# A two-layer streaming-encoder trunk: the norm's g applied with tokens on partitions, and latents normalised token tile by token tile

## The chip, the cores and the metric

The kernel runs on one core of a Trainium2 chip. The metric is the device time of one execution in microseconds (us); before the change its median over three runs is 704.25 us (703.63 to 704.76). The engines have their own instruction queues and meet through semaphores: TensorE (PE; its weight loads are listed as PEld), VectorE (DVE), ScalarE (ACT), GpSimd (POOL) and SyncE (SP), which here issues the DMAs.

## The reference

The input x is 512 tokens of 1024 numbers, float32. Each of two layers computes

```
h = rmsnorm(x) * norm_g[l]                       # over the 1024 features
p = split(h @ w_in[l])                           # 4040 columns
o_a = latent attention(p.a_cq, p.a_ckv, p.a_krope)
o_b = differential attention;  o_c = attention on the top 128 keys of an indexer;  o_d = short gated convolution
x = x + concat(o_a*silu(gate_a), o_b*..., o_c*..., o_d*...) @ w_out[l]
```

and at the end x is normalised once more, with final_g. In the latent attention the 256 columns a_cq and the 128 columns a_ckv of each token are normalised by their own root mean square, multiplied by their own g, and then by the small matrices w_uq (256 x 384) and w_ukv (128 x 512) to give queries, keys and values. The indexer needs 40 further columns of the same projection (one key of 32 and eight weights), and a_krope has 32.

## The kernel before

Products keep nearly full precision by splitting each operand into a high part (rounded by ACT's copy to the matmul's type) and a low part (the difference, by DVE or POOL), and adding three matmuls: high by high, high by low, low by high (`mm3`, L122). A helper on the way out of PSUM, `split_ps` (L112), does such a split with one ACT and one DVE instruction; `split_w` (L103) does it for a weight in SBUF with one ACT cast and subtractions of 256 columns on POOL.

Norm. `Norm` (L250) holds one tile of 128 tokens, tokens on partitions. `part` sums squares on ACT, `finish` makes the reciprocal root (ACT Sqrt, then a few DVE steps on 128x1) and multiplies the two halves of 512 columns, one on DVE (L287) and one on ACT (L288). In the layers g is not applied there: `Hidden.fill` (L296) transposes the tile to features on partitions, 128 by 128, eight times, two to a PSUM bank, and each 128-column split multiplies by g, which then is one number per partition (`gcol`, got by transposing norm_g once, L991 to L993). Only the final norm has g on tokens: POOL multiplies x by it early (L274).

First stage. Each layer begins with the 456 columns that the latents and the indexer need: for token tile t and weight quarter q, `first_part(q, t)` adds six matmuls into the tile's PSUM bank (tiles 0 and 1 in banks named proj, of which there are three, tiles 2 and 3 in banks named s). The order of norms (n), fills (e), weight splits (c) and parts is written out in `FIRST`. After quarter 3 ACT copies the bank to SBUF (L517, tile t1s).

Latents. `latent` (L583) then copies the indexer's columns out, sums the squares of all four tiles' latents (L599, L600), takes one reciprocal root over 128x8 numbers by integer steps on DVE (`rsqrt`, L136), multiplies (L608), transposes the latents (L616), splits them with their g per partition, builds the rotary key, loads and splits w_ukv (L647 to L655), multiplies by it (L656 on), then loads and splits w_uq and multiplies by that (L670 on). These matmuls are listed under L127 (`mm3`). `latent` runs merged with the first projections of the indexer and gates (`merge`, L229): the generators yield estimated costs, and the stream that is least far goes next, which fixes the program order.

Order and buffers. SP's order in the first stage of layer 0 is the written one. Elsewhere and on all other engines a planner orders instructions by readiness in its own cost model, earlier program order first, and hands out buffers from pools: 20 buffers of 512 KB named big, four raw weight buffers (`raw_tile`), four for split weights, seven named prob.

At the end of layer 0, `out_last` adds the last products to x, and `after` runs the next layer's norm and fills on each token tile beside it.

Of the kernel before, what the change touches and what calls it, by code (L numbers as in the profile page):

```python
# [19 lines left out]
P = 128  # L20
S = 512
D = 1024
# [43 lines left out]
def hybrid_trunk(ctx, tc, x_in, norm_g, w_in, qa_g, w_uq, kva_g, w_ukv, dlam, subg,  # L66
# [91 lines left out]
    grow = const.tile([DEPTH * KT, P], FT, name="grow")  # L158
    gcol = const.tile([P, DEPTH * KT], FT, name="gcol")
# [85 lines left out]
    def load_g(src):  # L245
        g = flat(big(FT))
        nc.sync.dma_start(g, src[None, :].to_broadcast([P, D]))
        return g

    class Norm:  # L250


        def __init__(self, x, g=None):
            self.x, self.g = x, g
            self.xn = flat(big(FT))
            self.ss = sm.tile([P, 4], FT, name="ss")
            self.n = 0

        def part(self, c):
# [11 lines left out]
            if self.g is not None:  # L271
# [4 lines left out]
        def finish(self):  # L276
# [9 lines left out]
            src = self.x if self.g is None else xn  # L286
            nc.vector.tensor_scalar(out=xn[:, :512], in0=src[:, :512], scalar1=r, scalar2=None, op0=OP.mult)  # L287
            nc.scalar.activation(xn[:, 512:], src[:, 512:], AF.Copy, scale=r)  # L288

    class Hidden:  # L290
        def __init__(self, l):
            self.l0 = l * KT
# [3 lines left out]
        def fill(self, t, xn):  # L296
            for g in range(4):
                b = bank("pt")
                for j in range(2):
                    k = 2 * g + j  # L300
                    nc.tensor.transpose(b[:, j * P:(j + 1) * P], xn[:, k * P:(k + 1) * P], ident)
                    split_ps(self.h[g][:, j, t * P:(t + 1) * P], self.l[g][:, j, t * P:(t + 1) * P],
                             b[:, j * P:(j + 1) * P], gcol[:, self.l0 + k:self.l0 + k + 1])
# [6 lines left out]
    def layer(l, hT, enter, after):  # L310
# [182 lines left out]
        t1s = [big(FT), big(FT)]  # L493
        t1 = lambda t, c0, c1: t1s[t // 2][:, t % 2, c0:c1]
# [14 lines left out]
        def first_part(q, t):  # L509
# [6 lines left out]
            if q == 3:  # L516
                nc.scalar.copy(t1(t, 0, 456), acc[t][:, :456])  # L517
# [64 lines left out]

        def latent():  # L583
            rep = prob()
            repv = rep.rearrange("p (t r c) -> p t r c", t=NT, r=4)
            for i in range(2):
                nc.vector.tensor_copy(repv[:, 2 * i:2 * i + 2],
                                      t1s[i][:, :, None, 416:448].to_broadcast([P, 2, 4, 32]))
            widx = A["widx"] = sm.tile([P, NT, 8], FT, name="widx", bufs=2)
            for i in range(2):  # L590
                nc.vector.tensor_copy(widx[:, 2 * i:2 * i + 2], t1s[i][:, :, 448:456])
# [4 lines left out]
            ss = sm.tile([P, NT, 2], FT, name="ssa")  # L596
            for t in range(NT):
                jk = prob()
                nc.scalar.activation(jk[:, :256], t1(t, 0, 256), AF.Square, accum_out=ss[:, t, 0:1])  # L599
                nc.scalar.activation(jk[:, 256:384], t1(t, 256, 384), AF.Square, accum_out=ss[:, t, 1:2])  # L600
# [485 lines left out]
```

## Time and profile before

| | before |
|---|---|
| median of three runs | 704.25 us |
| the profiled execution's own time | 706.75 us |
| its span, first to last instruction | 705.0 us |
| mean granted TensorE clock | 0.969 |
| PE / PEld busy | 637.8 / 538.9 us |
| DVE / ACT / POOL busy | 490.3 / 382.3 / 275.7 us |

The rest of this document reads one profiled execution. "Busy" is time in which an engine executes; register, branch and semaphore instructions don't count. Matmul ends are modelled, so a busy PE is not necessarily PE at its peak. The granted clock is the share of full speed that PE was given. A wait is put down to the semaphore that came last.

### The profile page before, as it was taken

The numbers are of one execution on the slowest core, as the hardware profiler recorded it, in microseconds if no ns is written. First come the engines' busy times: TensorE is split into PE (matmuls) and PEld (weight loads), VectorE is DVE, ScalarE is ACT, GpSimd is POOL, SyncE is SP. The second block draws the span as 40 slices with busy tenths as digits, with TensorE's granted clock in tenths as the row PEclk, the third lists the DMA queues.
The fourth block names the chain that finished last, engine by engine and source line by source line (L and its number), as shares of the span: only waits on it lengthen the run. The fifth ranks groups of instructions, "written<-read, shape, count | busy, mean of one in ns | idle before, by whom it ended". The sixth has DMA issues, their size and how long they took to land. (4 is left out here: it accounts for less than half of the span.)

```text
span 705.0 us, 11082 instructions
## 1 busy us (share of the span) xinstructions
PE 637.8 (90%) x3600; PEld 538.9 (76%) x3608; DVE 490.3 (70%) x1464; ACT 382.3 (54%) x910; POOL 275.7 (39%) x408
## 2 busy tenths in 40 slices
PE   3987999789999898999999779998999999999994
PEld 2675878678788677899978567887878986789994
DVE  4665664389999797645384846769999959664537
ACT  7673475376453455454387355866554345445435
POOL 3173333413533443343432543234353354334355
PEclk9997999899999999999999889999999999999998
DMA  7545265384457220234261653354533841023203
GB/s 226 120 119 160 64 121 136 110 177 120 101 130 218 69 82 32 70 140 113 57 195 32 181 149 94 113 145 109 129 90 91 223 113 46 22 67 143 91 1 119
DMA packets 86441, 79.67 MB, mean 113 GB/s; under 512 B 7286, under 2 KB 73400, under 8 KB 86384
## 3 DMA queue, kind: packets, MB, share of 16 engines
q1 hardware_dynamic: 86384, 78.98, 40.7%
q8 instruction: 28, 0.46, 0.3%
q14 instruction: 29, 0.24, 0.1%
HBM read 64.18 MB, written 12.16 MB: 108 GB/s over the span
## 5 line engine op out<-in xcount | busy, mean ns | idle before, releaser
L101 POOL TENSOR_TENSOR wl<-wr,wh 128x256 fp32r<-128x256 f32 (+1 forms) x304 | 224.2, 770 | 355.6 <-ACT wh L106 287.1
L127 PE MATMUL ps_proj<-big,wh 128*128 128x512 f32 x768 | 257.3, 409 | 1.3 <-DVE prob L471 1.0
L127 PE MATMUL ps_proj<-wh,big 128*128 128x256 f32 (+2 forms) x768 | 173.8, 312 | 2.1 <-DVE prob L762 1.3
L127 PEld LDWEIGHTS ps_proj<-big,wh 128*128 128x128 f32 x768 | 142.2, 194 | 26.0 <-DVE prob L471 1.4
L127 PE MATMUL ps_proj<-big,wl 128*128 128x512 f32 x384 | 153.6, 400 | 0.0
L127 PEld LDWEIGHTS ps_proj<-wh,big 128*128 128x128 f32 x768 | 129.8, 193 | 8.5 <-ACT big L118 1.6
L127 PE MATMUL ps_proj<-wl,big 128*128 128x256 f32 (+2 forms) x384 | 117.4, 306 | 1.1 <-DVE wl L108 1.0
L106 ACT CAST wh<-wr 128x1024 fp32r<-128x1024 f32 (+2 forms) x84 | 83.8, 998 | 36.5 <-PE ps_proj L127 19.9
L127 PEld LDWEIGHTS ps_proj<-big,wl 128*128 128x128 f32 x384 | 73.8, 192 | 14.6
L127 PEld LDWEIGHTS ps_proj<-wl,big 128*128 128x128 f32 x384 | 74.3, 194 | 4.8 <-DVE wl L108 2.1
L116 DVE TENSOR_TENSOR ptl<-ps_pt,pth 128x128 fp32r<-128x128 f32 (+1 forms) x96 | 46.6, 485 | 33.5 <-ACT pth L115 32.9
L115 ACT CAST pth<-ps_pt 128x128 fp32r<-128x128 f32 (+1 forms) x96 | 40.6, 425 | 46.3 <-PE ps_pt L413 45.9
L127 PE MATMUL ps_o<-pth,vt 128*128 128x256 f32 (+1 forms) x288 | 60.9, 283 | 4.7 <-ACT pth L115 3.2
L477 ACT ACTIVATE prob<-ps_s,st_a 128x128 f32<-128x128 f32 (+1 forms) x64 | 33.9, 530 | 45.1 <-DVE st_a L489 29.6
L127 PEld LDWEIGHTS ps_o<-pth,vt 128*128 128x128 f32 x288 | 49.9, 198 | 9.8 <-ACT pth L115 6.3
L413 PE MATMUL ps_pt<-ident,prob 128*128 128x128 f32 x240 | 43.2, 279 | 11.6 <-ACT prob L481 8.9
L574 DVE MATCH_REPLACE8 ia<-m,ia 128x256 f32<-128x256 f32 (+2 forms) x96 | 52.0, 545 | 0.1
L573 DVE MAX8 m<-ia 128x8 f32<-128x256 f32 (+2 forms) x96 | 50.8, 551 | 1.0 <-POOL ia L565 0.8
L127 PE MATMUL ps_o<-ptl,vt 128*128 128x256 f32 (+1 forms) x144 | 42.8, 297 | 6.0 <-DVE ptl L116 6.0
L413 PEld LDWEIGHTS ps_pt<-ident,prob 128*128 128x128 f32 x240 | 28.5, 140 | 23.8 <-ACT prob L481 14.5
L481 ACT ACTIVATE prob<-prob,st_a 128x128 f32<-128x128 f32 (+1 forms) x64 | 35.8, 564 | 10.8 <-DVE st_a L480 10.7
L115 ACT CAST vt<-ps_proj 128x128 fp32r<-128x128 f32 x48 | 12.3, 265 | 46.8 <-PE ps_proj L127 29.1
(159 smaller groups left out, 1000.2 us busy)
## 6 DMA issues: line engine op xcount, KB each, us to landing
wr<-in_w_in_dram SPq DMA_DIRECT2D x56, 512.0 KB
big<-trip SPq DMA_DIRECT2D x64, 128.0 KB
trip<-big SPq DMA_DIRECT2D x28, 256.0 KB
big<-in_x_dram SPq DMA_DIRECT2D x7, 512.0 KB
wr<-in_w_in_dram SPq DMA_DIRECT2D x8, 416.0 KB
big<-trip SPq DMA_DIRECT2D x32, 96.0 KB
wr<-in_w_out_dram SPq DMA_DIRECT2D x8, 384.0 KB
big<-big SPq DMA_DIRECT2D x8, 256.0 KB
```

Source lines behind the costliest of these rows:

```text
L101: nc.gpsimd.tensor_tensor(out=o[:, c], in0=a[:, c], in1=b[:, c], op=OP.subtract)
L106: nc.scalar.copy(h[:, :n], raw[:, :n])
L115: nc.scalar.copy(hi, src)
L116: nc.vector.tensor_tensor(out=lo, in0=src, in1=f(hi), op=OP.subtract)
L127: nc.tensor.matmul(o, lhsT=a, rhs=b, start=start and i == 0 and j == 0, stop=stop and i == n - 1 and j == 2, skip_group_check=skip)
L413: nc.tensor.transpose(b[:, k * P:(k + 1) * P], p[:, k * P:(k + 1) * P], ident)
L477: nc.scalar.activation(p[:, :W], s[:, :W], AF.Exp, scale=-1.0, bias=mn, accum_out=sums)
L481: nc.scalar.activation(p[:, :W], p[:, :W], AF.Copy, scale=st[:, 2:3])
L573: nc.vector.max(out=m8, in_=a)
L574: nc.vector.match_replace(out=a, in_to_replace=m8, in_values=a, imm_value=MARK)
```

## The change

Four things are edited. The norm's g is loaded for all 128 partitions and applied where tokens are on partitions: `finish` now computes x * r * g with two DVE steps of 512 columns (the final norm keeps its early multiplication on POOL). The g tiles of the layers sit in raw weight buffers; layer 0's is loaded behind the first token tile of x, and a Sqrt on one column is executed at the very start. `fill` splits two transposed blocks, 256 columns, at once and without a scale. Each token tile's latents are normalised by `first_norm` straight from its PSUM bank behind its last matmul, with ACT's Sqrt in place of the integer steps; only the other 72 columns are copied out. And w_ukv is loaded and split by `latent_weights` at the start of `latent`. The diff, with lines of context only where needed:

```diff
...
     pcol = const.tile([P, 20], FT, name="pcol")
-    grow = const.tile([DEPTH * KT, P], FT, name="grow")
-    gcol = const.tile([P, DEPTH * KT], FT, name="gcol")
     subs = const.tile([P, DEPTH], FT, name="subs")
...
-    def load_g(src):
-        g = flat(big(FT))
+    def load_g(src, g=None):
+        g = flat(big(FT)) if g is None else g
         nc.sync.dma_start(g, src[None, :].to_broadcast([P, D]))
...
-        def __init__(self, x, g=None):
-            self.x, self.g = x, g
+        def __init__(self, x, g, early=False):
+            self.x, self.g, self.early = x, g, early
             self.xn = flat(big(FT))
...
                                                    in1=ss[:, n - 1:n], op0=OP.mult, op1=OP.add)
-            if self.g is not None:
+            if self.early:
                 for a in range(c.start, c.stop, PIECE):
...
             nc.vector.scalar_tensor_tensor(out=r, in0=t, scalar=1.5, in1=r, op0=OP.add, op1=OP.mult)
-            src = self.x if self.g is None else xn
-            nc.vector.tensor_scalar(out=xn[:, :512], in0=src[:, :512], scalar1=r, scalar2=None, op0=OP.mult)
-            nc.scalar.activation(xn[:, 512:], src[:, 512:], AF.Copy, scale=r)
+            if not self.early:
+                for c in (slice(0, 512), slice(512, D)):
+                    nc.vector.scalar_tensor_tensor(out=xn[:, c], in0=self.x[:, c], scalar=r, in1=self.g[:, c],
+                                                   op0=OP.mult, op1=OP.mult)
+                return
+            nc.vector.tensor_scalar(out=xn[:, :512], in0=xn[:, :512], scalar1=r, scalar2=None, op0=OP.mult)
+            nc.scalar.activation(xn[:, 512:], xn[:, 512:], AF.Copy, scale=r)
...
     class Hidden:
-        def __init__(self, l):
-            self.l0 = l * KT
+        def __init__(self):
             self.h = [big() for _ in range(KT // 2)]
...
                     nc.tensor.transpose(b[:, j * P:(j + 1) * P], xn[:, k * P:(k + 1) * P], ident)
-                    split_ps(self.h[g][:, j, t * P:(t + 1) * P], self.l[g][:, j, t * P:(t + 1) * P],
-                             b[:, j * P:(j + 1) * P], gcol[:, self.l0 + k:self.l0 + k + 1])
+                c = slice(t * P, (t + 1) * P)
+                split_ps(self.h[g][:, :, c], self.l[g][:, :, c], b[:, :2 * P].rearrange("p (j c) -> p j c", j=2))
...
-        t1s = [big(FT), big(FT)]
-        t1 = lambda t, c0, c1: t1s[t // 2][:, t % 2, c0:c1]
+        t1 = sm.tile([P, NT, 72], FT, name="t1", bufs=1)
+        cn = [flat(big(FT)), flat(big(FT))]
...
             if q == 3:
-                nc.scalar.copy(t1(t, 0, 456), acc[t][:, :456])
+                first_norm(t, acc[t])
+        def first_norm(t, a):
+            w = sm.tile([P, 8], FT, name="ssa")
+            m, r, u = w[:, 0:2], w[:, 2:4], w[:, 4:6]
+            jk = prob()
+            for c, (c0, c1) in enumerate(((0, 256), (256, 384))):
+                nc.scalar.activation(jk[:, c0:c1], a[:, c0:c1], AF.Square, scale=(c1 - c0) ** -0.5,
+                                     accum_out=m[:, c:c + 1])
+            nc.vector.tensor_scalar(out=m, in0=m, scalar1=EPS, scalar2=None, op0=OP.add)
+            nc.scalar.activation(r, m, AF.Sqrt)
+            nc.scalar.copy(t1[:, t], a[:, 384:456])
+            nc.vector.reciprocal(out=r, in_=r)
+            nc.vector.tensor_tensor(out=u, in0=r, in1=r, op=OP.mult)
+            nc.vector.scalar_tensor_tensor(out=u, in0=u, scalar=-0.5, in1=m, op0=OP.mult, op1=OP.mult)
+            nc.vector.scalar_tensor_tensor(out=r, in0=u, scalar=1.5, in1=r, op0=OP.add, op1=OP.mult)
+            for c, (c0, c1) in enumerate(((0, 256), (256, 384))):
+                nc.vector.tensor_scalar(out=cn[t // 2][:, (t % 2) * 512 + c0:(t % 2) * 512 + c1], in0=a[:, c0:c1],
+                                        scalar1=r[:, c:c + 1], scalar2=None, op0=OP.mult)
...
+        def latent_weights():
+            raw = raw_tile()
+            nc.sync.dma_start(raw[:, :512], w_ukv[l])
+            w = big()
+            kh, kl = w[:, 0, :], w[:, 1, :]
+            rk = raw[:, :512].rearrange("p (h b c) -> p b h c", h=4, b=2)
+            nc.scalar.copy(kh.rearrange("p (b h c) -> p b h c", h=4, b=2), rk)
+            for b in range(2):
+                c = slice(b * 256, (b + 1) * 256)
+                nc.gpsimd.tensor_tensor(out=kl[:, c].rearrange("p (h c) -> p h c", h=4), in0=rk[:, b],
+                                        in1=f(kh)[:, c].rearrange("p (h c) -> p h c", h=4), op=OP.subtract)
+            A["ukv"] = kh, kl
         def latent():
+            latent_weights()
             rep = prob()
             repv = rep.rearrange("p (t r c) -> p t r c", t=NT, r=4)
-            for i in range(2):
-                nc.vector.tensor_copy(repv[:, 2 * i:2 * i + 2],
-                                      t1s[i][:, :, None, 416:448].to_broadcast([P, 2, 4, 32]))
+            nc.vector.tensor_copy(repv, t1[:, :, None, 32:64].to_broadcast([P, NT, 4, 32]))
             widx = A["widx"] = sm.tile([P, NT, 8], FT, name="widx", bufs=2)
-            for i in range(2):
-                nc.vector.tensor_copy(widx[:, 2 * i:2 * i + 2], t1s[i][:, :, 448:456])
+            nc.vector.tensor_copy(widx, t1[:, :, 64:72])
             b = rep_turn(rep)
...
             nc.vector.tensor_tensor(out=kst[64:P], in0=b[64:P], in1=f(kst)[64:P], op=OP.subtract)
-            ss = sm.tile([P, NT, 2], FT, name="ssa")
-            for t in range(NT):
-                jk = prob()
-                nc.scalar.activation(jk[:, :256], t1(t, 0, 256), AF.Square, accum_out=ss[:, t, 0:1])
-                nc.scalar.activation(jk[:, 256:384], t1(t, 256, 384), AF.Square, accum_out=ss[:, t, 1:2])
-            for c, n in ((0, 256), (1, 128)):
-                nc.vector.tensor_scalar(out=ss[:, :, c], in0=ss[:, :, c], scalar1=1.0 / n, scalar2=EPS,
-                                        op0=OP.mult, op1=OP.add)
-            ra = rsqrt(ss.rearrange("p t c -> p (t c)"), 2 * NT)
-            cn = [flat(big(FT)), flat(big(FT))]
-            for t in range(NT):
-                for c, (c0, c1) in enumerate(((0, 256), (256, 384))):
-                    nc.vector.tensor_scalar(out=cn[t // 2][:, (t % 2) * 512 + c0:(t % 2) * 512 + c1], in0=t1(t, c0, c1),
-                                            scalar1=ra[:, 2 * t + c:2 * t + c + 1], scalar2=None, op0=OP.mult)
             yield CH[0]
...
             tb = sm.tile([P, NT, 16], FT, name="ropb", bufs=1)
-            for i in range(2):
-                x1, x2 = t1s[i][:, :, 384:400], t1s[i][:, :, 400:416]
-                tt = slice(2 * i, 2 * i + 2)
-                co, si = ctok[:, tt, 0:16], ctok[:, tt, 16:32]
-                nc.vector.tensor_tensor(out=ta[:, tt], in0=x2, in1=si, op=OP.mult)
-                nc.vector.tensor_tensor(out=tb[:, tt], in0=x1, in1=si, op=OP.mult)
-                nc.vector.tensor_tensor(out=r2[:, tt, 0, 0:16], in0=x1, in1=co, op=OP.mult)
-                nc.vector.tensor_tensor(out=r2[:, tt, 0, 16:32], in0=x2, in1=co, op=OP.mult)
+            x1, x2 = t1[:, :, 0:16], t1[:, :, 16:32]
+            co, si = ctok[:, :, 0:16], ctok[:, :, 16:32]
+            nc.vector.tensor_tensor(out=ta, in0=x2, in1=si, op=OP.mult)
+            nc.vector.tensor_tensor(out=tb, in0=x1, in1=si, op=OP.mult)
+            nc.vector.tensor_tensor(out=r2[:, :, 0, 0:16], in0=x1, in1=co, op=OP.mult)
+            nc.vector.tensor_tensor(out=r2[:, :, 0, 16:32], in0=x2, in1=co, op=OP.mult)
             nc.vector.tensor_tensor(out=r2[:, :, 0, 0:16], in0=r2[:, :, 0, 0:16], in1=ta, op=OP.subtract)
...
-            raw = raw_tile()
-            nc.sync.dma_start(raw[:, :512], w_ukv[l])
-            kh, kl = (w[:, i, :] for w in (big(),) for i in range(2))
-            rk = raw[:, :512].rearrange("p (h b c) -> p b h c", h=4, b=2)
-            nc.scalar.copy(kh[:, :512].rearrange("p (b h c) -> p b h c", h=4, b=2), rk)
-            for b in range(2):
-                c = slice(b * 256, (b + 1) * 256)
-                nc.gpsimd.tensor_tensor(out=kl[:, c].rearrange("p (h c) -> p h c", h=4), in0=rk[:, b],
-                                        in1=f(kh)[:, c].rearrange("p (h c) -> p h c", h=4), op=OP.subtract)
+            kh, kl = A["ukv"]
             for j in range(2):
...
         ctx.enter_context(tc.manual_schedule(engines=INORDER))
-    h = Hidden(0)
+    h = Hidden()
     x0 = {}
+    g0 = raw_tile()
+    warm = sm.tile([P, 1], FT, name="warm", bufs=1)
+    nc.scalar.activation(warm, ident[:, 0:1], AF.Sqrt)
...
         elif what == "s":
-            if t == 0:
-                b = bank("pt")
-                nc.tensor.transpose(b[:, :DEPTH * KT], grow, ident[:DEPTH * KT, :DEPTH * KT])
-                nc.vector.tensor_copy(gcol, b[:, :DEPTH * KT])
             x0[t].part(slice(0, 512))
...
             if t == 0:
-                nc.sync.dma_start(grow, norm_g.rearrange("l (k p) -> (l k) p", p=P))
-            x0[t] = Norm(x)
+                load_g(norm_g[0], g0)
+            x0[t] = Norm(x, g0)
...
             if t == 0 and c.start == 0:
-                st["g"] = load_g(final_g) if l + 1 == DEPTH else None
+                st["g"] = load_g(final_g) if l + 1 == DEPTH else load_g(norm_g[l + 1], raw_tile())
                 if l + 1 < DEPTH:
-                    st["h"] = Hidden(l + 1)
+                    st["h"] = Hidden()
             if c.start == 0:
-                st["n"].append(Norm(x, st["g"]))
+                st["n"].append(Norm(x, st["g"], l + 1 == DEPTH))
             norm = st["n"][t]
...
```

## Rows read from the trace of the kernel before

**Rows 1.** The page's first part: busy us, share of the span, instructions.

```profile
PE 637.8 (90%) x3600; PEld 538.9 (76%) x3608; DVE 490.3 (70%) x1464; ACT 382.3 (54%) x910; POOL 275.7 (39%) x408
```

**Rows 2.** Waits of TensorE: in total us, how often, longest us.

```profile
PE ps_pt L616 <- DVE big L608: 8.9, 4, 4.0
...
PE ps_proj L127 <- POOL big L654: 4.6, 2, 2.3
...
PE ps_proj L127 <- ACT big L651: 2.2, 2, 1.5
```

**Rows 3.** Windows: stretch, length, busy by engine (PE, PEld, DVE, ACT, POOL), clock, DMA, GB/s.

```profile
5.00:10.00 5.00, 0.00 (x0) 0.00 (x0) 2.19 (x9) 3.69 (x7) 1.47 (x2) 1.00 1.03 339
...
25.00:43.00 18.00, 18.00 (x92) 14.57 (x91) 8.91 (x27) 12.58 (x30) 7.36 (x11) 1.00 0.26 59
...
55.00:60.00 5.00, 5.00 (x16) 4.15 (x17) 3.37 (x9) 1.26 (x2) 0.00 (x0) 0.50 0.75 209
...
68.00:73.30 5.30, 5.30 (x13) 4.15 (x14) 2.75 (x4) 3.20 (x10) 4.00 (x9) 0.50 0.42 107
...
130.00:140.00 10.00, 5.68 (x29) 4.71 (x29) 5.17 (x9) 4.88 (x10) 7.34 (x10) 0.75 0.44 135
...
400.40:404.80 4.40, 4.39 (x16) 3.52 (x16) 2.61 (x5) 1.38 (x2) 0.00 (x0) 0.51 0.67 198
...
413.00:418.30 5.30, 5.30 (x13) 4.15 (x14) 2.75 (x4) 3.20 (x10) 4.03 (x9) 0.50 0.40 102
...
470.00:480.00 10.00, 8.54 (x48) 6.82 (x47) 7.04 (x20) 6.41 (x16) 5.09 (x11) 1.00 0.92 222
```

**Rows 4.** Timeline of 48 to 56 us: start, length, instruction, idle before it.

```profile
48.35 5.54 POOL L101 TENSOR_TENSOR wl<-wr,wh 128x256 fp32r<-128x256 f32 x8 [4.26 <-ACT wh L106]
...
51.23 0.65 DVE L145 TENSOR_TENSOR rs_t<-rs_y 128x8 f32<-128x8 f32 x1
...
54.15 0.17 DVE L147 SCALAR_TENSOR_TENSOR rs_y<-rs_t,rs_y 128x8 f32<-128x8 f32 x1
...
54.96 1.12 PE L616 MATMUL ps_pt<-ident,big 128*128 128x128 f32 x4 [3.99 <-DVE big L608]
```

**Rows 5.** Groups by line and shape: count, busy us, mean ns, idle before.

```profile
L599 ACT ACTIVATE prob<-big 128x256 f32<-128x256 f32 x8 | 3.3, 413 | 0.1
...
L280 ACT ACTIVATE nw<-ss 128x1 f32<-128x1 f32 x12 | 3.5, 288 | 0.1
...
L280 ACT ACT_TABLE_LOAD x3 | 3.8, 1283 | 0.1
...
L118 ACT ACTIVATE big<-ps_pt,gcol 128x128 fp32r<-128x128 f32 x64 | 22.0, 366 | 9.9 <-PE ps_pt L301 9.5
...
L115 ACT CAST pth<-ps_pt 128x256 fp32r<-128x256 f32 x24 | 9.0, 373 | 4.6 <-PE ps_pt L413 4.5
...
L287 DVE TENSOR_SCALAR big<-big,nw 128x512 f32<-128x512 f32 x12 | 7.6, 633 | 1.7 <-PE ps_pt L301 1.2
...
L288 ACT ACTIVATE big<-big,nw 128x512 f32<-128x512 f32 x12 | 8.5, 718 | 4.4 <-DVE nw L285 3.4 <-DVE ss L266 1.0
...
L845 DVE SCALAR_TENSOR_TENSOR prob<-prob,gate 128x512 f32<-128x512 f32 x4 | 3.1, 773 | 0.1
```

**Rows 6.** Timeline around the latents of layer 0.

```profile
25.32 0.34 SPq L648 DMA_DIRECT2D wr<-in_mla_w_ukv_dram  x1
...
43.04 0.71 PE L127 MATMUL ps_proj<-big,wh 128*128 128x512 f32 x2
...
72.62 0.60 POOL L682 TENSOR_TENSOR big<-wr,big 128x64 fp32r<-128x64 f32 x2 [0.18 <-ACT big L681]
...
77.87 2.89 PE L127 MATMUL ps_proj<-big 128*128 128x512 f32 x12
```

**Rows 7.** Timeline of the start.

```profile
10.54 1.26 DVE L287 TENSOR_SCALAR big<-big,nw 128x512 f32<-128x512 f32 x1
...
11.86 0.69 PE L301 MATMUL ps_pt<-ident,big 128*128 128x128 f32 x2 [7.13 <-DVE nw L283]
```

## The prediction

> **What bounds the kernel now.** I read the busy time first [rows 1]: TensorE (PE) is busy for 637.8 of 705.0 us, the others for 70% or less. So time can only come out of PE's idle 67.2 us, out of stretches in which PE is slow, or out of its work, and the change leaves every matmul and transpose of the layers in place. Then I read who PE waits for [rows 2]. Three of the largest totals belong to what the change touches: transposes of the normalised latents (L616) wait 8.9 us for the multiplies at L608, and the first latent matmuls (L127 on the tile of w_ukv) wait 4.6 us for POOL's L654 and 2.2 us for ACT's L651. That is 15.7 us, both layers together; 7.1 us more are PE's wait for the first normalised token tile [rows 7]. Third, the granted clock by windows [rows 3]: right behind each pair of these waits PE runs at 0.50 of full speed (1.2 instead of 2.4 GHz), in four stretches of 5.0, 5.3, 4.4 and 5.3 us. In them PE counts as busy for nearly all of the time, so the busy share does not show this loss. Last, what the transposes wait for [rows 4]: PE has nothing from 50.97 to 54.96 us (3.99 us) while DVE goes through the reciprocal root of all four token tiles, one small instruction after the other, each 0.65 us while POOL is subtracting beside it and 0.17 us once POOL is done.
>
> **The change, part by part.**
>
> *Latents by token tile.* Gone after the last tile of the first stage are the copy L517, eight squares, eleven small DVE steps on 128x8 and eight multiplies. In their place each tile has its own chain behind its last matmul: two squares, an add, a root, four small DVE steps, two multiplies, and a 72-column copy. Three of the four chains run beside the other tiles' matmuls. The last one is on the path: two squares of at most 0.413 each [rows 5], together 0.8; add 0.17 to 0.65, root 0.29 [rows 5], four small steps 0.17 to 0.65 each [rows 4], two multiplies of 256 and 128 columns from PSUM, at most the 0.77 of a 512-column DVE step each, about 0.7 together [rows 5]. Sum 2.6 us without POOL beside it, 5.0 with. What covers it is the projection PE begins at 43.04 us [rows 6] and goes on with until 50.97, that is 7.9 us. So the wait at L616 goes. Nothing is late behind it as long as the planner leaves the transposes where they stand, and with the wait goes the slow stretch behind it. The squares wait on ACT for the tile's last matmul, as L517 did; queued behind them are the casts of later projections, which PE takes up only after the first one. The accumulators are held for the length of the chain instead of one copy, two of the three proj banks among them; the third carries the first projection, and the second one asks for its bank some 5.5 us later.
>
> The root is a new kind of work beside an exponential. In the trace each change of function set is an ACT_TABLE_LOAD of 1.283 us [rows 5], and in layer 0 the exponentials of the lambda parameters become ready just then. If they fall between two tiles' roots, two more loads, 2.57 us, lengthen the chain to at most 7.6 us, still under 7.9. The Trainium skill, "ScalarE: Activation LUTs", section "Table sets: the hidden batching unit", speaks against this edit: exp and sqrt sit in different sets, so mixing them costs a load each way, about 2.7 us per switch with its drain. By its figure the chain would be about 10.4 us in layer 0, an estimate, and PE would wait about 2.5 us there; by the rows it would wait for nothing.
>
> *w_ukv prepared first.* The load stands on SP's queue at 25.32 us already [rows 6]; the copy and the two subtractions come only where PE waits for them. Moved ahead, one copy and two subtractions per layer run while PE is full (25 to 43 us: PE 18.00 of 18.00, ACT 12.58, POOL 7.36 [rows 3]), so they cost nothing there, and the waits of 4.6 and 2.2 us go with the slow stretches behind them. On SP it now stands ahead of the projections' weights and takes one of the four raw buffers earlier, but gives it back earlier too. Late next would be w_uq: its last two subtractions begin at 72.62 and PE takes it up at 77.87 [rows 6]. Without the waits (2.3 and 0.7 us here [rows 2]) and the 2.65 lost to the clock PE would be there at about 72.2. But two of POOL's subtractions ahead of it (0.7 each, as 5.54 us for eight in [rows 4]) are gone too, so the last two would begin at about 71.2 and end 0.6 later: covered, by some 0.4 us, which is the thinnest cover of the forecast.
>
> *Splits of 256 columns.* Per layer 32 pairs of ACT and DVE become 16. ACT, both layers: 64 x 0.366 = 23.4 us becomes 32 x 0.373 = 11.9 [rows 5], DVE alike. That stage is bound by PE [rows 3], so I count 0; below, up to 1 us gained per layer where PE starts it.
>
> *The norm with g.* One DVE multiply (0.633) and one ACT multiply (0.718) per tile become two DVE steps of about 0.77 [rows 5], 1.5 us instead of 0.7 on the way to a tile's second half, on DVE, which in that stage is half idle. Beside out_last and the first stage PE has other work; 0. The transpose of g and its copy go; they were not waited for beyond the first tile.
>
> *The start of layer 0.* Between x's first tile and the first weights, SP's queue gets a load of 512 KB (g for all partitions) in place of 8 KB. DMA is full there (1.03 of its engines, 339 GB/s [rows 3]), so every later load lands 512 KB / 339 GB/s = 1.5 us later. Against it, the extra table load of 1.283 us at the first root goes (the warm-up asks for that set first), and the first tile is normalised at 10.54 to 11.80 only because of DVE's order. Ends: 3 us gained, if DVE takes the first tile up when its root is known; 3 us lost, if the 1.5 us pass through and the two steps run as long as the 1.26 us that the first multiply took [rows 7]. I take 1.5 lost, the row of DMA.
>
> *Layer 1's g* takes a raw buffer from out_last until the last tile is normalised. With three left, the fourth first-stage weight comes a buffer later. Between 0, if it takes the first weight's buffer, and a wait like that at L616, if it waits for g's; the loads of that stage land long before use, so 0.
>
> **Sum**, against the profiled execution (span 705.0 us, 706.75 us with what lies around it, 2.5 above the median of 704.25): 15.7 us of waits, and half of 5.0 + 5.3 + 4.4 + 5.3 = 20.0, that is 10.0 us, of clock; together 25.7. New small waits in the two latent stages I take at what PE has elsewhere: 67.2 - 11.9 (start) - 15.7 = 39.6 us in some 690, or 0.57 per 10 us; over two latent stages of some 33 us, 3.8. So 706.75 - 25.7 + 3.8 + 1.5 = 686.35, and 2.5 lower on the scale of the median: **684 us**. Its own range: 676 (no new waits, start 3 gained) to 691 (start 3 lost, one new wait of 3 us with 2.5 of clock).
>
> **Rivals.**
> *One pair of waits comes back* (0.25). Either the w_uq cover of 0.4 us fails, or the table loads and contention hold the last chain beyond 7.9 us. A wait of a few us has the slow clock behind it in all four rows, so it costs what it did: second pair 6.8 + 5.3 = 12.1, first pair 8.9 + 4.7 = 13.6. Time 696 to 698. For it: both covers are thin, and DVE's small steps are four times as long beside POOL. Against it: POOL and ACT were idle ahead of both places. A rule from the Trainium skill bears on the first: "SBUF — State Buffer", section "Who interferes with whom", says that a DVE step with two SBUF inputs contends with POOL's reads; the rows agree (0.65 against 0.17), and three of the new chain's steps are of that kind.
> *The change doesn't do what it says* (0.05): the order is the planner's on all engines but SP, and it could put transposes and w_ukv where they wait as before: 704, only the start moves.
> *Slower* (0.09): the planner orders and hands out buffers anew, and later stages get waits as in 130 to 140 us, where PE idles 4.3 us and loses 2.5 to the clock (mean 0.75); the same stage in layer 1, 470 to 480, idles 1.5 at full clock [rows 3]. That is 5.3 us per place between a good and a bad order of the same code. From four such places on, the gain is gone (684 + 21 = 705); with five it is 711. For it: that pair of rows. Against: the code of those stages isn't touched, and everything in them only moves forward.
>
> **How the numbers follow.** Likeliest 0.61, one pair back 0.25, no effect 0.05, slower 0.09. The range that holds 8 of 10 runs from just under the likeliest's lower end, 675, to beyond the second case, 699. What can be told from no change is 0.2%, 1.4 us: faster by more 0.86, within 0.05, slower 0.09.
>
> **What would show it.** Right: no PE wait for the multiplies ahead of L616's counterpart; matmuls of the w_ukv tile without a wait for POOL or ACT; clock at 1.00 through the two latent stages (43 to 75 and 387 to 420 us), which shrink by about 11 us each; nothing of this lost later. Wrong: a wait of over 2 us of PE on w_uq's subtraction, on the last tile's chain or on the fourth weight of layer 1's first stage; the first transpose later than 13.4 us; or the latent stages shorter and the stages behind them longer by as much.

## The result and the profile after

The changed kernel takes 679.75 us (median of four runs, 678.9 to 680.8) against 704.5 us for the kernel before, measured beside it on the same chip: a ratio of 0.9651, 95% interval 0.9635 to 0.9668. The forecast was 684, with 675 to 699 as its range.

The first part of the page after: busy time, share of the span and instructions, as in [rows 1].

```profile
span 678.0 us, 11037 instructions
...
PE 622.1 (92%) x3599; PEld 533.6 (79%) x3607; DVE 487.4 (72%) x1441; ACT 364.6 (54%) x879; POOL 278.5 (41%) x408
```

The span is 27.0 us shorter. PE's idle time fell by 11.3 us (67.2 to 55.9) and its busy time by 15.7, though it does the same matmuls: part of that is the clock, whose mean rose from 0.969 to 0.990, and 5.5 us are the transposes of the normalised tiles (L301, now L302: 18.4 to 12.9 us busy).

TensorE's waits after, to set beside [rows 2].

```profile
PE ps_pt L302 <- DVE big L286: 13.8, 1, 13.8
...
PE ps_proj L127 <- DVE big L116: 2.1, 1, 2.1
PE ps_pt L634 <- DVE big L119: 1.4, 1, 1.4
PE ps_pt L544 <- DVE ssa L532: 1.4, 1, 1.4
```

L634 is the old L616, the transposes of the latents. Its 8.9 us of waiting for the multiplies are gone; what it waits for now, once, is a split by DVE (1.4). The matmuls on w_ukv wait for neither ACT nor POOL. New are 2.1 us for a split by DVE (L116) and 1.4 us at L544, which transposes the indexer's key; three more new waits have 0.8 us each. The first transposes wait until 13.84 us instead of 11.86.

Windows after: the counterparts of the latent stages in [rows 3] (41 to 77 and 376 to 412), then a stage the change does not touch, and a place in layer 1's first stage. Columns as in [rows 3].

```profile
41.00:61.00 20.00, 18.36 (x91) 14.33 (x91) 15.93 (x52) 12.63 (x28) 11.53 (x16) 1.00 0.67 182
61.00:77.00 16.00, 16.00 (x76) 13.40 (x75) 12.96 (x24) 9.67 (x26) 7.65 (x12) 1.00 0.57 167
120.00:130.00 10.00, 7.22 (x41) 6.71 (x39) 3.47 (x5) 2.39 (x5) 4.47 (x7) 0.66 0.58 163
350.00:355.00 5.00, 2.99 (x14) 2.62 (x15) 4.68 (x11) 2.10 (x7) 2.09 (x2) 0.84 0.73 234
355.00:360.00 5.00, 5.00 (x26) 4.35 (x24) 4.00 (x9) 2.00 (x5) 1.76 (x2) 0.82 0.57 138
376.00:396.00 20.00, 17.22 (x88) 13.91 (x87) 15.25 (x29) 10.84 (x21) 13.46 (x20) 1.00 0.79 219
396.00:412.00 16.00, 16.00 (x77) 13.38 (x76) 12.48 (x21) 10.52 (x26) 8.96 (x14) 1.00 0.42 125
```

The clock is 1.00 through both latent stages: the four stretches at 0.50 are gone with the waits ahead of them. The stage of 130 to 140 us in [rows 3], now at 120, still dips (0.66): nothing there was changed. New is the pair at 350 to 360: PE idles 2.0 us and the clock falls to 0.82.

To see where the 27.0 us came from, I read the same matmuls off both timelines and took the time between them (us). "e3" is an experiment told below.

| from one mark to the next | before | after | e3 |
|---|---|---|---|
| start to the first transpose | 11.86 | 13.84 | 10.96 |
| to the last 456-column matmul of layer 0's first stage | 30.89 | 27.20 | 30.85 |
| to the first score matmul on 100 partitions (L720, now L728), the latent stage | 46.69 | 35.48 | 35.46 |
| to layer 1's first 456-column matmul | 272.47 | 272.44 | 272.80 |
| to its last | 25.51 | 27.47 | 25.61 |
| to layer 1's first score matmul, the latent stage | 46.91 | 35.44 | 36.82 |
| to the first matmul with the ones (L781, now L789) in layer 1 | 114.59 | 112.43 | 112.54 |
| to the last of these | 72.06 | 69.71 | 69.73 |
| to the end | 84.02 | 83.99 | 84.03 |

The latent stages give 11.2 and 11.5 us, as forecast. The start costs 2.0, layer 0's first stage gives 3.7, layer 1's first stage costs 2.0. In a second execution of the changed kernel, where the clock does not fall there, layer 1's first stage takes 25.84 us and costs 0.3. Two stages of layer 1 that the change doesn't touch give 2.2 and 2.3. In the first of them PE idles 4.0 us instead of 5.9; in the second the kernel before has a slow stretch, 606.0 to 609.5 us at 0.52, and the changed kernel is at 1.00 throughout.

### The profile page after: what moved, and what is told of

The parts are those of the page before. It is cut to its first block, busy times and chain, and to the rows that moved or that the text cites. A ratio compares the mean times of both kernels' runs of the same rounds, so it can differ in the third digit from the quotient of the medians.

```text
span 678.0 us, 11037 instructions
## 1 busy us (share of the span) xinstructions
PE 622.1 (92%) x3599; PEld 533.6 (79%) x3607; DVE 487.4 (72%) x1441; ACT 364.6 (54%) x879; POOL 278.5 (41%) x408
## 4 chain that ended last, share of the span: by engine, by line
PE 58%; DVE 26%; ACT 7%; DMA 5%; issue 2%; POOL 1%; SPq 0%; ACTq 0%; DVEq 0%; POOLq 0%
PE ps_proj L127 43%; PE ps_o L127 5%; DVE ia L595 5%; DVE m L594 4%; PE ps_pt L414 3%; PE ps_s L127 2%; DMA wr<-in_w_in_dram 2%; DVE ptl L116 2%; DVE big L119 1%; DVE ps_s L490 1%; ACT prob L478 1%; DMA big<-in_x_dram 1%; PE ps_pt L302 1%; ACT prob L482 1%; DVE ia L581 1%
## 5 line engine op out<-in xcount | busy, mean ns | idle before, releaser
L101 POOL TENSOR_TENSOR wl<-wr,wh 128x256 fp32r<-128x256 f32 (+1 forms) x304 | 226.8, 779 | 326.1 <-ACT wh L106 279.4
L127 PE MATMUL ps_proj<-big,wh 128*128 128x512 f32 x768 | 250.7, 401 | 2.1 <-DVE prob L472 1.0
L127 PEld LDWEIGHTS ps_proj<-big,wh 128*128 128x128 f32 x768 | 138.8, 189 | 26.8 <-issue 1.5
L127 PE MATMUL ps_proj<-big,wl 128*128 128x512 f32 x384 | 151.7, 395 | 0.0
L127 PEld LDWEIGHTS ps_proj<-big,wl 128*128 128x128 f32 x384 | 72.3, 188 | 14.2
L116 DVE TENSOR_TENSOR ptl<-ps_pt,pth 128x128 fp32r<-128x128 f32 (+1 forms) x96 | 46.5, 485 | 31.4 <-ACT pth L115 30.8
L581 DVE SCALAR_TENSOR_TENSOR ia<-prob,widx,ia 128x256 f32<-128x256 f32 (+2 forms) x42 | 26.2, 639 | 12.7 <-ACT prob L576 12.0
```

What stands on the lines that cost most here:

```text
L101: nc.gpsimd.tensor_tensor(out=o[:, c], in0=a[:, c], in1=b[:, c], op=OP.subtract)
L116: nc.vector.tensor_tensor(out=lo, in0=src, in1=f(hi), op=OP.subtract)
L127: nc.tensor.matmul(o, lhsT=a, rhs=b, start=start and i == 0 and j == 0, stop=stop and i == n - 1 and j == 2, skip_group_check=skip)
L581: nc.vector.scalar_tensor_tensor(out=a, in0=r[:, :W], scalar=w, in1=a, op0=OP.mult, op1=OP.add)
```

## Experiments

**e1 and e2: the two parts on the latents, each alone.** e1 is the kernel before with `first_norm`; e2 is the kernel before with `latent_weights` at the head of the latent stage.

```diff
e1, on e3 below:
         def latent():
-            latent_weights()
...
+            latent_weights()
             kh, kl = A["ukv"]
e2, on the kernel before:
         def latent():
+            latent_weights()
...
-            raw = raw_tile()
-            nc.sync.dma_start(raw[:, :512], w_ukv[l])
...
+            kh, kl = A["ukv"]
```

> The kernel before with one part alone: latents normalised by token tile from PSUM. Theory (two pairs of waits, each with the slow clock behind it, add up): PE's 8.9 us at the latents' transposes and some 4.7 us of clock behind them go, so 13.6 us less: about 691. The waits for w_ukv's copy and subtraction (2.2 and 4.6 us) stay at their size. Rival 1 (one queue): the copy and the subtraction of w_ukv come no earlier on ACT and POOL, so PE, which gets there earlier, waits longer by as much: 699 to 704. Rival 2 (the norm with g and the wide splits carry part of the gain): 694 or more.

Measured: 693.53 us, ratio 0.9838 (0.9819 to 0.9856), so 11.0 less instead of 13.6. Rival 2 began at 694, half a microsecond away; e3 decides against it.

> The kernel before with one part alone: w_ukv loaded, copied and subtracted at the head of the latent stage. Theory: the waits of 4.6 and 2.2 us go with 5.3 us of clock, 12.1 us less: about 692; the wait at the transposes stays at 8.9 us. Rival 1 (one queue): POOL's two subtractions now stand beside DVE's chain of small steps, which sets the wait at the transposes; that wait grows by as much as the other falls: 699 to 704. Rival 2: 694 or more.

Measured: 692.39 us, ratio 0.9817 (0.9799 to 0.9836): 12.2 less, and 12.1 was forecast. That the number is so close is luck in part. In the trace the two latent stages are 6.3 and 3.8 us shorter, 10.1 together; 4.4 more come from the two later stages of layer 1 that also shrank in the changed kernel, and were not in the sum. (The trace is 14.5 us shorter in all, as that of before is 2.5 above its median.)

TensorE's waits in the two latent stages of e1 (43 to 75 us, then 380 to 410).

```profile
PE ps_proj L127 <- ACT big L609: 3.0, 1, 3.0
PE ps_pt L543 <- DVE prob L619: 0.9, 1, 0.9
PE ps_proj L127 <- DVE big L536: 0.7, 1, 0.7
...
PE ps_proj L127 <- POOL big L612: 2.3, 1, 2.3
PE ps_pt L543 <- DVE prob L619: 1.9, 1, 1.9
PE ps_proj L127 <- ACT big L609: 1.5, 1, 1.5
```

The wait at the transposes is gone. Those on w_ukv are 6.8 us in both layers together, as before (4.6 + 2.2 in [rows 2]), only more of them is for ACT now; so rival 1 is out. What the expectation left out are the new small waits that the part brings with it, 0.9 + 0.7 + 1.9 = 3.5 us (L543 transposes the indexer's key, L536 is a multiply of the new chain). 13.6 - 3.5 is 10.1, near the 11.0 measured, but the sum is not closed: in the trace the two latent stages are 6.9 and 5.1 us shorter, and start and layer 0's first stage 0.9.

The same view of e2 (43 to 70 us, then 380 to 410).

```profile
PE ps_pt L630 <- DVE big L622: 2.5, 1, 2.5
PE ps_proj L127 <- DVE big L116: 1.2, 1, 1.2
...
PE ps_pt L630 <- DVE big L622: 4.8, 1, 4.8
```

w_ukv's waits are gone. The wait for the multiplies has not grown (2.5 + 4.8 = 7.3, from 8.9); rival 1 is out for this part too.

**e3: both parts, with the old norm. e4: the rest alone.** e3 takes `first_norm`, the small `t1` and `latent_weights`, and keeps gcol, splits of 128 columns and the old start. e4 is the other half of the diff, with the latents as before.

```diff
e3, kept as before:
                     split_ps(self.h[g][:, j, t * P:(t + 1) * P], self.l[g][:, j, t * P:(t + 1) * P],
                              b[:, j * P:(j + 1) * P], gcol[:, self.l0 + k:self.l0 + k + 1])
e4, kept as before:
             if q == 3:
                 nc.scalar.copy(t1(t, 0, 456), acc[t][:, :456])
```

> Both parts on the latents, with the old norm (g as a column after the transposes, splits of 128 columns, no load of g at the start). Theory: they carry all of the change's 24.75 us: 13.6 + 12.1 = 25.7 less, 679 to 680, the same as the changed kernel within 1.4 us; the changed kernel's trace shows its start 2.0 us later, layer 0's first stage 3.9 us shorter and layer 1's 2.2 us longer, which is nothing in sum. Rival 2 (norm and splits carry part): 682 to 686. Rival 3 (norm, splits and g cost more than they give): 675 to 678.

Measured: 680.49 us, ratio 0.9653 (0.9636 to 0.9669). The theory holds: the two parts carry 24.1 of the 24.75 us, and the changed kernel (0.9651) can't be told from this one. 11.0 and 12.2 alone add up to 23.2, so they are nearly independent. The latent stages alone say the same: 11.9 and 10.1 us shorter in e1 and e2, 21.3 in e3.

> The rest of the change alone: g on tokens, splits of 256 columns, load of g at the start, latents and w_ukv as before. Theory: 704.5 within 1.4 us: first transpose 2.0 us later, layer 0's first stage 3.9 us shorter, layer 1's 2.2 us longer by a wait of 2 to 3 us on a split behind the norm. Rival 2: 699 to 702. Rival 3: 706 to 709.

Measured: 707.88 us, ratio 1.0039 (1.0022 to 1.0056), runs from 704.68 to 709.55. The theory missed: the rest alone costs about 2.8 us by the ratio, and the time lies in rival 3's range. Its profiled execution (706.53 us, span 704.8) shows only why nothing is gained: layer 0's first stage ends 2.4 us earlier, and the latent stage behind it, with its old wait for the multiplies, is 2.3 longer; every other stage is within 0.5 us of before. Layer 1's first stage has the expected wait (2.2 us) and is only 0.3 longer, at full clock. Where the other executions lost time stays open. On top of the latents (e3 to the changed kernel) the same edits cost nothing.

**e10: narrow splits in the changed kernel.** What in the rest does what?

```diff
-                c = slice(t * P, (t + 1) * P)
-                split_ps(self.h[g][:, :, c], self.l[g][:, :, c], b[:, :2 * P].rearrange("p (j c) -> p j c", j=2))
+                    split_ps(self.h[g][:, j, t * P:(t + 1) * P], self.l[g][:, j, t * P:(t + 1) * P],
+                             b[:, j * P:(j + 1) * P])
```

> The changed kernel with splits of 128 columns again (32 pairs of ACT and DVE per layer instead of 16), the norm with g on tokens kept. Theory (the wide splits shorten layer 0's first stage, 26.1 us from its first to its last matmul of 456 columns against 30.0 before): the stage goes back to 29 to 30 us, and layer 1's, 25.8 to 27.5 now, grows by 1 to 3, since DVE's queue there gets longer still: 683 to 687. Rival 1 (the norm's form shortens it: no ACT step, no g in the splits): the stage stays at 26 to 27 and the time within 1.4 us of 679.7. Rival 2 (stage longer, but later stages give it back): stage at 29 to 30, time 679 to 682.

Measured: 685.16 us, ratio 0.972 (0.970 to 0.974). Layer 0's first stage goes from 26.1 to 28.2 us, layer 1's to 28.9. The theory holds in time and in direction; 28.2 is short of its 29 to 30. Not all of the shortening from 30.0 to 26.1 is the wide splits', then: 1.8 us of it is there without them. So the rest is two effects of opposite sign: by the ratios, g on tokens with its load costs 0.972 - 0.9653, some 4.7 us, and the wide splits give back 0.972 - 0.9651, some 4.9, each uncertain by some 1.8 us by the intervals. Their near cancelling is why e3 and the changed kernel agree.

What the wide splits save is PE's own time. The transposes of the normalised tiles in the kernel before, in e10 and in the changed kernel, columns as in [rows 5]:

```profile
L301 PE MATMUL ps_pt<-ident,big 128*128 128x128 f32 x64 | 18.4, 295 | 7.6 <-DVE nw L283 7.1 <-DVE ss L266 0.4
...
L302 PE MATMUL ps_pt<-ident,big 128*128 128x128 f32 x64 | 17.8, 302 | 16.2 <-DVE big L286 14.0 <-DVE big L116 2.2
...
L302 PE MATMUL ps_pt<-ident,big 128*128 128x128 f32 x64 | 12.9, 304 | 13.8 <-DVE big L286 13.8
```

The same 64 transposes, each about as long, keep PE busy for 4.9 us less in the changed kernel than in e10 (in e3 it is 18.2 us). With wide splits they all come two or four in a row and overlap: two usually take 0.38 us, four 0.60. With narrow ones 46 of them (58 in e3) stand alone between matmuls, mostly 0.27 us each. PE's whole busy time differs by 3.6 us (625.7 in e10, 622.1).

**e6, e7 and e8: what makes the new wait of 2.1 us in layer 1.** A timeline of the changed kernel around it: start, length, instruction, idle before it.

```profile
344.68 1.42 DVE L286 SCALAR_TENSOR_TENSOR big<-big,nw,wr 128x512 f32<-128x512 f32 x2
...
346.74 0.46 DVE L281 TENSOR_TENSOR nw<-nw 128x1 f32<-128x1 f32 x1
...
347.67 0.57 DVE L282 SCALAR_TENSOR_TENSOR nw<-nw 128x1 f32<-128x1 f32 x1
...
348.71 0.68 DVE L283 SCALAR_TENSOR_TENSOR nw<-nw 128x1 f32<-128x1 f32 x1
...
349.43 2.20 DVE L286 SCALAR_TENSOR_TENSOR big<-big,nw,wr 128x512 f32<-128x512 f32 x2
349.48 0.38 PE L302 MATMUL ps_pt<-ident,big 128*128 128x128 f32 x2
...
351.55 0.74 DVE L116 TENSOR_TENSOR big<-ps_pt,big 128x256 fp32r<-128x256 f32 x2
...
352.01 0.48 PE L127 MATMUL ps_proj<-wh,big 128*128 128x456 f32 x1 [2.15 <-DVE big L116]
```

PE goes on transposing the first tile at 349.48, and the split it then needs (L116) stands on DVE behind the third tile's two multiplies by g, 2.20 us beside POOL (the second tile's took 1.42 with POOL idle). e6 takes the multiplies by g away, and with them g's load and its raw buffer; e7 gives POOL more to do; e8 changes the order.

```diff
e6, in after(), and in finish() for layer 1:
-                st["g"] = load_g(final_g) if l + 1 == DEPTH else load_g(norm_g[l + 1], raw_tile())
+                st["g"] = load_g(final_g) if l + 1 == DEPTH else None
...
+            if self.g is None:
+                nc.vector.tensor_scalar(out=xn[:, :512], in0=self.x[:, :512], scalar1=r, scalar2=None, op0=OP.mult)
+                nc.scalar.activation(xn[:, 512:], self.x[:, 512:], AF.Copy, scale=r)
+                return
e7:
-FM = (456, 456)
+FM = (456, 0)
e8, in after():
+            if l + 1 < DEPTH and t >= 2:
+                st["h"].fill(t - 2, st["n"][t - 2].xn)
             norm.finish()
             if l + 1 < DEPTH:
                 nc.sync.dma_start(xs[t * P:(t + 1) * P, :], x)
-                if t >= 2:
-                    st["h"].fill(t - 2, st["n"][t - 2].xn)
```

> The changed kernel without the multiplication by g at layer 1 (left out of the computation), with one DVE step on 512 columns and one ACT step on the rest per tile, as before the change; wide splits kept. Theory (the norm with g on DVE makes layer 1's stall): PE's waits of 2.1 and 0.8 us on the splits go, layer 1's first stage falls from 27.5 to 24 to 25.5 us, time 675 to 677.5. Rival (the wide splits make it: a tile's transposes give PE only half as many releases): the waits stay, 679 to 680.

Measured: 676.96 us, ratio 0.9616 (0.9584 to 0.9648). The waits of 2.1 and 0.8 go (the longest left in the stage is 0.4); the stage is 24.2 us. The time alone would not decide: the interval reaches that of the changed kernel. The wide splits don't make the stall.

> The changed kernel with layer 1's first weights subtracted by POOL alone (912 columns each) instead of half by DVE and half by POOL. Theory (contention: DVE's steps are slow while POOL subtracts): POOL's stretch at 346 to 352 us gets about twice as long, DVE's small steps of the norm stay at 0.46 to 0.68, PE's wait on the split grows to 3 us or more: 681 to 684. Rival (length of DVE's queue): DVE has two steps of 0.62 less ahead of the split that PE waits for, the wait falls to about 1 us: 677 to 679.

Measured: 679.91 us, ratio 0.9659 (0.9621 to 0.9697). Neither number came: the wait is the same 2.1 us, and the stage 27.7. DVE's queue in e7 ahead of the split that PE waits for, and POOL beside it:

```profile
347.84 4.85 POOL L101 TENSOR_TENSOR wl<-wr,wh 128x256 fp32r<-128x256 f32 x6 [12.13 <-ACT wh L106]
...
349.33 0.66 DVE L283 SCALAR_TENSOR_TENSOR nw<-nw 128x1 f32<-128x1 f32 x1
350.03 2.08 DVE L286 SCALAR_TENSOR_TENSOR big<-big,nw,wr 128x512 f32<-128x512 f32 x2
352.03 0.41 DVE L116 TENSOR_TENSOR big<-ps_pt,big 128x256 fp32r<-128x256 f32 x1
```

The norm's small steps, now back to back, still take 0.66 us beside POOL, and the same two multiplies, 2.08 us, stand ahead of the split; what POOL does longer lies behind this place. So e7 could not separate the two causes as it was meant to.

> The changed kernel with the transposes and splits of tile t-2 written ahead of the norm of tile t at the border of the layers. Theory (DVE's queue: the split that PE waits for stands behind the two steps with g of the next tile, 2.20 us beside POOL): PE's waits of 2.1 and 0.8 us in layer 1's first stage go, and with them some 2.2 us of slow clock behind; that stage is 27.5 us long and falls to 24 to 25.5: 675 to 677.5. Rival (contention: DVE's steps are long because POOL subtracts beside them, 0.46 to 0.68 instead of 0.15, wherever they stand): a wait of 2 us or more comes back at another split and the time stays at 679 to 680.

Measured: 676.03 us, ratio 0.9597 (0.9578 to 0.9616), against 0.9647 (0.9624 to 0.9670) for the changed kernel beside it. DVE's queue in e8:

```profile
345.20 1.41 DVE L286 SCALAR_TENSOR_TENSOR big<-big,nw,wr 128x512 f32<-128x512 f32 x2
346.53 0.42 DVE L116 TENSOR_TENSOR big<-ps_pt,big 128x256 fp32r<-128x256 f32 x1
...
347.92 0.48 DVE L281 TENSOR_TENSOR nw<-nw 128x1 f32<-128x1 f32 x1
```

The split of the first tile now runs at 346.53, while PE is still at the last matmuls of layer 0, and PE's longest wait in the stage is 0.7 us for a DVE split. The stage is 23.8 us long. The slow small steps beside POOL are still there (0.48 instead of 0.15) and cost nothing. So the new order is enough to end the stall, and the rival is out: no wait comes back elsewhere. That does not make contention small. In the changed kernel it lengthens what stands ahead of the split by an estimated 2 us, by the rows above: 1.2 in the three small steps (0.46, 0.57 and 0.68 instead of about 0.15 each) and 0.8 in the multiplies. That is about the whole wait. Whether the old order would have cost anything with POOL idle there is not shown.

**The changed kernel again, e5 and e9: the start.** e5 issues g's load behind x's second tile; e9 has that and e8's order.

```diff
-            if t == 0:
+            if t == 1:
                 load_g(norm_g[0], g0)
```

> The changed kernel itself, as the measure on this chip for the three beside it: 679.75 within 1.4 us.

Measured: 679.68 us, ratio 0.9647.

> The changed kernel with the load of layer 0's g issued behind x's second tile instead of ahead of the first weights. Theory (the 512 KB ahead of the weights set the start): w0's cast back at about 7.5 us instead of 9.82, x's second tile back at 8.8 instead of 11.15, first transpose at 11.9 to 12.4 instead of 13.84, and the 1.5 to 2 us pass through to the end: 677.7 to 678.3. Rival (layer 0's first stage, now 26.1 us long, ends when its last weights and splits are there, whenever it starts): first transpose earlier, but the stage ends at 41.0 as before and the time stays at 679 to 680.

Measured: 680.38 us, ratio 0.9665 (0.9644 to 0.9686). The rival holds: the first transpose comes at 12.32 us instead of 13.84, but the first stage behind it takes 28.16 instead of 27.20 us, so 0.6 us is left of 1.5 where the stage ends; PE now waits 1.1 us there for ACT's cast of a weight. Even 0.6 is not clear of chance: in six other profiles with the changed kernel's start the first transpose comes between 13.05 and 14.23 us, and in the five of them that have the wide splits the stage ends between 40.36 and 41.52, against 40.48 here. In the profiled execution, at 683.3 us the slowest of four, time was also lost to the clock, in stages that the edit doesn't touch (below).

> The two edits together (g's load behind x's second tile, transposes ahead of the next norm). Theory: the sums add up, 1.5 to 2 and 2.2 to 4.7: 673 to 676. Rival: only one of them counts, 677 to 678.5, or none, 679 to 680.

Measured: 675.26 us, ratio 0.9582 (0.9562 to 0.9601). The number lies in the theory's range, but not by its sum: e8 alone gives 3.5 us and e5 alone nothing that can be told. Only the order at the border of the layers counts: start and first stage together end at 40.97 us, at 41.28 in e8. e8 and e9 beat both kernels; they can't be told from each other.

## Why the prediction was right, and where it was not

**The waits of 15.7 us.** Right. All three rows of [rows 2] are gone, and e1 to e3 put 24.1 of the 24.75 us on the two edits that were to remove them.

**The clock, 10.0 us.** Right in kind: clock 1.00 in both latent stages. Waits, clock and the new small waits (3.8) made 21.9 of the forecast, for both stages; the table has 22.7. The new waits measured 4.4 us (PE busy 35.58 of the 40 us in the two 20-us windows above).

**The last tile's chain.** The result was right, the size wrong, and luck had a part. I gave it 2.6 to 5.0 us, 7.6 with two table loads. In layer 0 it took 8.6, from the last 456-column matmul's end at 41.04 to the last multiply's end, more than the 7.9 that I had as cover. On ACT its squares begin only at 43.23, behind an earlier tile's root. DVE's part of it:

```profile
45.64 0.15 DVE L532 RECIPROCAL ssa<-ssa 128x2 f32<-128x2 f32 x1
...
45.91 0.70 DVE L533 TENSOR_TENSOR ssa<-ssa 128x2 f32<-128x2 f32 x1
46.54 0.21 DVE L647 TENSOR_TENSOR ropb<-t,ctok 128x64 f32<-128x64 f32 x1
46.67 0.69 DVE L534 SCALAR_TENSOR_TENSOR ssa<-ssa 128x2 f32<-128x2 f32 x1
47.40 0.69 DVE L627 TENSOR_TENSOR kst<-ps_pt,kst 64x512 fp32r<-64x512 f32 x1
48.12 0.64 DVE L535 SCALAR_TENSOR_TENSOR ssa<-ssa 128x2 f32<-128x2 f32 x1
...
48.93 0.74 DVE L537 TENSOR_SCALAR big<-ps_s,ssa 128x256 f32<-128x256 f32 x2
```

I had counted the chain's own steps as if they followed each other. On DVE the other tiles' chains, the rope's steps and kst's subtraction stand between them, and three steps are slow beside POOL (0.64 to 0.70, as [rows 4] had it). The transposes (L634) came at 50.43 us, 0.8 later than the chain's end at 49.67 and with no wait. So it was covered, but by 0.8 us, not by the 2.9 to 5.3 that I had argued, and only because PE itself had waited 1.6 us in between, 0.79 and 0.85. The first of these is the bank that I had taken to be free: the first projection waits at 42.00 for a multiply of an earlier tile's chain (L537) to give up a proj bank. Without the two waits PE would have come at about 48.8, by my estimate, before the chain's end.

**Table loads.** The risk did not come. Six loads of 1.28 us before and six after; the load for layer 0's exponentials moved from 42.11 to 58.59 us, behind all roots of the latents. The Trainium skill, "ScalarE: Activation LUTs", section "Table sets: the hidden batching unit", has about 2.7 us for a load; with two of them the chain would have been some 10.4 us by my estimate. No run here shows a switch inside the chain; where this trace shows one, at 4.96 us, the load takes 1.28 and the root follows at 6.26.

**w_ukv early.** Right: its waits are gone in e2 and in the changed kernel. That e2's 12.2 met the 12.1 is partly luck, as told there. w_uq, my thinnest cover, had none of PE's waits: PE is busy for 16.00 of the 16.00 us from 61 to 77.

**Splits of 256 columns, 0 to 1 us gained per layer.** Wrong, the largest miss. e10 shows some 4.9 us: 2.1 in layer 0's first stage, 1.4 in layer 1's against the first execution (3.0 against the second), the rest behind. The stage is nearly bound by PE, as I had it, though less ahead of the window of 25 to 43 us in [rows 3]: from 12 to 32 us PE is busy for 18.2 of 20 us before the change. What failed is the premise that PE's work stays the same because the change leaves every transpose in place. The transposes of the normalised tiles fell from 18.4 to 12.9 us of PE's time, and where PE is the limit, that is time gained.

**Norm with g on tokens, 0.** Wrong too, in the other direction: with the start, some 4.7 us (e10 against e3); in the two traces 1.2 of it lies ahead of the end of layer 0's first stage and 3.2 in layer 1's. I named PE's cover and not DVE's queue. At the border of the layers e6 shows 2.2 us of it (0.9647 - 0.9616, with an interval of 2.3 to either side) and e8 3.5 (0.9647 - 0.9597). The wait of 2.1 us there was in none of my lists, and the step that failed is "beside out_last and the first stage PE has other work; 0".

**The start, +1.5.** First transpose +1.98 us (between profiles it varies by 0.9 us with the old start and by 1.2 with the new); but it is not passed on whole (e5, e9). "The extra table load goes" was wrong: the warm-up root was executed at 10.68 us, behind the first real root, and both loads are still there. It cost nothing against before: there the first root's load stood at 4.93 us, here at 4.96. I had set "later than 13.4" as a sign of being wrong; 13.84 was that sign, for this term alone.

**Layer 1's g in a raw buffer, 0.** Right: the fourth weight of that stage was loaded a buffer later (issued at 348.25 us), and PE waited for none of its splits.

**The sum.** The trace fell by 27.0 us where I had 20.4. The two latent stages were 0.8 off. The other 5.8: layer 0's first stage 3.7, layer 1's -2.0, the start -0.5, and 4.6 from the later stages, chiefly the two of 2.2 and 2.3 us. These two show in e2, e3 and all kernels made from the changed one, not in e4, and in e1 only the second, with 1.6 us. Of the first, 1.9 us is idle time of PE, and of the second 1.7 is the slow stretch at 606 us; why they went was not sought and stays open. No term of mine had them, so the mechanism that I forecast does not explain this part of the gain. As the profiled execution of before was 2.5 us above its median and that of after on it, the medians differ by 24.75.

## What to carry to other kernels

A wait with a slow stretch behind it is worth both, and two such pairs in different queues add up; look for them in the waits and the clock's windows before any busy share. Cost a chain of small steps by the queue they stand in, not by their own lengths. And when a step moves to another engine, look at what stands behind it in that engine's order: writing the waited-for work ahead of it (e8) was worth as much, within the noise, as taking the step away (e6).

## What the runs showed of the hardware

The same wait does not cost the same clock each time. After PE's wait of 2.1 to 2.2 us at 350 us in layer 1 the clock fell for part of the ten us from 350 in one execution of the changed kernel (0.84 and 0.82, shown above), not at all in the second, and in e5 to its lower level, 1.2 GHz, for all of 355 to 360. Windows of the second execution, then of e5:

```profile
350.00:355.00 5.00, 2.84 (x18) 2.31 (x17) 4.99 (x12) 1.96 (x7) 2.71 (x3) 1.00 0.65 197
355.00:360.00 5.00, 5.00 (x31) 4.45 (x30) 4.80 (x13) 2.44 (x6) 1.76 (x2) 1.00 0.73 194
```

```profile
140.00:145.00 5.00, 5.00 (x20) 4.32 (x20) 3.60 (x8) 4.10 (x11) 1.37 (x2) 0.50 0.00 0
225.00:230.00 5.00, 3.67 (x13) 3.01 (x14) 3.11 (x13) 2.67 (x8) 0.39 (x1) 0.74 0.76 202
350.00:355.00 5.00, 2.04 (x10) 1.39 (x10) 5.00 (x10) 1.84 (x6) 4.39 (x5) 0.87 0.53 145
355.00:360.00 5.00, 5.00 (x19) 4.25 (x17) 3.16 (x11) 2.79 (x7) 0.42 (x1) 0.50 0.63 192
```

In these the stage took 27.47, 25.84 and 28.71 us, with waits there that differ by 0.1. The first two rows of e5 are places where the changed kernel's clock is 1.00. A gain of 1 to 2 us at one place can thus be hidden by where the clock happens to fall, as e5's was; several executions are needed to see it.
